# A two-layer hybrid mixing block: a fourth buffer for two weight rings, spectra products from split parts, and an early output projection in two rounds

## The chip, the cores and the metric

The kernel runs on one core of one Trainium2 chip. The metric is the device time of one execution in microseconds; it is told as the median of several runs. The engines are named as in the profile: PE is TensorE (matmul; PEld its weight loads), DVE is VectorE, ACT is ScalarE, POOL is GpSimd, SP is SyncE, which here only issues transfers.

## The reference

Two layers work on 512 latent tokens and 256 context tokens of width 1024. Each layer has a token mixing part with four groups of heads, which share an input and an output projection, and a feed-forward part. In short:

```python
for l in range(2):
    need_ctx = l < 1
    mod  = silu(c) @ ada_w[l] + ada_b[l]          # shifts, scales, gains; the same for ctx
    h, hc = modulate(rmsnorm(x)), modulate(rmsnorm(ctx))
    pl, pc = h @ w_in, hc @ w_in                  # 1024 -> 2400
    # four groups of 256 columns of the mixed result
    y = concat(s5(pl, pc), hyena(pl), retention(pl, pc), mla(pl, pc)) @ w_out
    x = x + g1 * rmsnorm(y)
    x = x + g2 * rmsnorm(conv_ffn(modulate(rmsnorm(x))))   # w_up 1024x5632, conv, silu gate, w_down
    # the same for ctx in layer 0
# hyena: z = x1 * long_conv(v, 0); z = x2 * long_conv(z, 1), with filter spectra
def hyena_spectra(n, w1, b1, w2, b2, w3, freq, deltas):
    hid = sin(freq * (z @ w1 + b1));  hid = sin(freq * (hid @ w2 + b2))   # 64 wide
    k = (hid @ w3) * exp(-t01 * abs(deltas))      # n x (2 orders x 2 directions x 256)
    k = k * rsqrt(sum(k * k)); return rfft(two_sided(k))
```

All values are float32.

## The kernel before, in words

Activations stand transposed, with channels on partitions and tokens along the free axis: segment 0 is the context (256 tokens), segment 1 the latents (512). A dense product takes weights of 128x128 as the stationary side and tokens as the moving side.

**Split products.** A float32 matmul of the tensor engine is slow, so most large products are made from split parts in the type F32R. `load_w` (line 308) brings a weight block of 128x1024 (512 KB) from memory into the raw ring "wr" (`load_raw`, line 299), ACT casts it to a high part "wh" (`split_w`, line 305), and DVE subtracts to get the low part "wl" (line 306). "wr", "wh" and "wl" have three buffers each. Activations are split in the same manner into H1h and H1l (latents), H0h and H0l (context). `passes` (line 320) gives three products for each block k: wh by high, wh by low, wl by high. `dense` (line 329, its products on line 341) is built on it. Weight loads are issued at a raised priority, so that they go ahead of other work in the order. A second ring, "ar", of three buffers of 128x1024 too, holds adaLN weights (`ada`, line 461; its products on line 482), the Fourier tables of the hyena part (lines 822 and 880) and some others.

**What sets the order.** The code is written as Python generators that take turns (`weave`, `ahead`): a list of input projection jobs, a chain with retention, S5 and the context's hyena part, a chain with latent attention (MLA) and, in layer 0, the latents' hyena part, the spectra, and the adaLN products. How many steps each takes in a turn is a table of small numbers. From what is written this way a scheduler lays out one list of instructions for each engine, and an engine works its list off in order: an instruction that waits holds all behind it. Nearly all transfers are issued by SP, in SP's order; GpSimd issues the loads of S5's operands (lines 991 and 992) and some of MLA's (lines 1379 and 1381).

**Spectra** (`hy_spectra`, line 744). Two small products with a sine after each give the hidden layer h2 of 64 rows and n columns. For both orders, w3 (64x512) is loaded, and for each of the T2 = n/128 token blocks one float32 product (line 790) makes 128x512 filter values, which are multiplied by a window, squared and summed, normed, and transformed. This is done for the context and the latents of layer 0 beside the input projection of layer 0 (60 to 340 us), and for the latents of layer 1 beside the feed-forward part of layer 0 (912 to 1003 us).

**The hyena loop** (line 879). For each pair of frequencies a table tb comes into "ar", a spectrum kt from memory; lines 890 and 891 transform forwards, DVE multiplies (lines 894 to 899), and `back` (lines 872 and 873) transforms back for the pair before.

**S5's readout** reloads what it stored before (lines 1075 and 1076, tiles A_U and A_T) and works on it on DVE (line 1077).

**The early output projection** (`early_out`, line 1816, its products on line 1827). When the results of a head group stand in C (the split tiles H1h, H1l, H0h, H0l of the mixed result, blocks k: 0 and 1 S5, 2 and 3 hyena, 4 and 5 retention, 6 and 7 MLA), part of the output projection can be done. In layer 0, where `stage[0]` is set, this starts when all of KP = (4, 5, 0, 1, 6, 7) is filled. Three blocks of w_out are loaded, and seven sums of 18 products of 256 columns each are begun in four PSUM tiles, 126 products. The blocks 2 and 3 and the rest of the columns follow in the main output projection (line 1898).

The scratch for descriptors of GpSimd's transfers has its default size, since the program's constructor names none; it lies in the on-chip memory that the pools share.

## Time and profile before

| | us |
|---|---|
| three runs | 2066.98, 2062.43, 2060.63 |
| median | 2062.43 |
| the profiled execution | 2065.18 |
| its span | 2063.4 |
| TensorE busy | 1891.1 (92%) |
| VectorE busy | 1330.3 (64%) |
| ScalarE busy | 791.3 (38%) |
| GpSimd busy | 173.3 (8%) |
| mean granted clock of TensorE | 0.951 |

Busy time is summed over the instructions of an engine; the granted clock is a share of full speed, so 1.00 stands for 2.4 GHz and 0.50 for 1.2 GHz, and values between are means over a stretch. The stages of the span: 0 to 340 us adaLN and the input projection of layer 0 with spectra, S5's preparation and retention beside it; 340 to 612 us the rest of mixing in layer 0 (MLA, S5, hyena, early output projection); to about 710 us the output projection; then the feed-forward part of layer 0 until about 1240 us; mixing of layer 1 until about 1690 us; its feed-forward part to the end. Idle time in the profile stands in brackets at the instruction that came after it, with what released it.

### The profile page before, as it was taken

How to read it: one execution, taken by the hardware profiler on the slowest of the kernel's cores; microseconds unless marked ns; L12 is line 12 of the kernel's file. 1: busy time of each engine (PE TensorE's matmuls, PEld its weight loads, DVE VectorE, ACT ScalarE, POOL GpSimd, SP SyncE). 2: the span in 40 equal slices, each digit the busy share in tenths (PEclk: the TensorE clock that was granted, in tenths of full speed). 3: DMA queues.
4: the chain of work that ended last, by engine and by line, in shares of the span. 5: the costliest groups of instructions: out<-in, count | busy, mean ns of one | idle time of the engine just before them, and what ended most of it. 6: DMA issues, size and time to landing. Idle time of an engine off the chain costs nothing. (4 is left out here: it accounts for less than half of the span.)

```text
span 2063.4 us, 29216 instructions
## 1 busy us (share of the span) xinstructions
PE 1891.1 (92%) x11142; PEld 1554.8 (75%) x11142; DVE 1330.3 (64%) x2488; ACT 791.3 (38%) x1351; POOL 173.3 (8%) x195
## 2 busy tenths in 40 slices
PE   6898999887899899999999998889989979999996
PEld 1766666566698788878888887678867968888885
DVE  4767463686746897776788447538767555555555
ACT  3646312343334434352523233433355534333332
POOL 0221004100001002100000001110022000000001
PEclk8899999889999999999999999899989989999998
DMA  8557456635452543333277222486621423333331
GB/s 287 179 191 236 159 167 181 152 84 159 133 175 93 195 126 114 123 97 103 87 276 253 64 77 74 117 213 197 196 84 51 144 88 116 103 92 102 93 102 41
DMA packets 147411, 284.96 MB, mean 138 GB/s; under 512 B 35429, under 2 KB 78598, under 8 KB 147272
## 3 DMA queue, kind: packets, MB, share of 16 engines
q1 hardware_dynamic: 139592, 274.70, 41.8%
q0 software_dynamic: 3072, 7.08, 2.0%
q10 hardware_dynamic: 4608, 1.31, 0.3%
q8 instruction: 88, 1.44, 0.3%
q14 instruction: 51, 0.42, 0.1%
HBM read 231.17 MB, written 48.99 MB: 136 GB/s over the span
## 5 line engine op out<-in xcount | busy, mean ns | idle before, releaser
L306 DVE TENSOR_TENSOR wl<-wr,wh 128x1024 fp32r<-128x1024 f32 x174 | 214.0, 1232 | 262.4 <-ACT wh L305 259.7
L341 PE MATMUL mm<-H1h,wh 128*128 128x512 f32 x888 | 354.8, 399 | 5.5 <-DVE st L426 4.5
L341 PE MATMUL mm<-H1h,wl 128*128 128x512 f32 x888 | 353.8, 399 | 0.3 <-DVE wl L306 0.3
L341 PE MATMUL mm<-H1l,wh 128*128 128x512 f32 x888 | 351.8, 396 | 0.0
L305 ACT CAST wh<-wr 128x1024 fp32r<-128x1024 f32 x174 | 182.2, 1050 | 354.6 <-PE mm L341 295.2
L341 PEld LDWEIGHTS mm<-H1h,wh 128*128 128x128 f32 x888 | 168.4, 190 | 47.0 <-issue 6.5
L341 PEld LDWEIGHTS mm<-H1l,wh 128*128 128x128 f32 x888 | 168.0, 189 | 38.7 <-issue 2.6
L341 PEld LDWEIGHTS mm<-H1h,wl 128*128 128x128 f32 x888 | 168.2, 189 | 37.2 <-issue 0.8
L341 PE MATMUL mm<-H0h,wh 128*128 128x256 f32 x480 | 137.0, 285 | 9.9 <-DVE st L426 9.9
L404 POOL TENSOR_TENSOR rq_y<-rq_v,halves 128x2 f32<-128x2 f32 (+3 forms) x37 | 36.0, 972 | 1233.8 <-DVE rq_v L403 736.9
L341 PE MATMUL mm<-H0l,wh 128*128 128x256 f32 x480 | 138.2, 288 | 0.0
L341 PE MATMUL mm<-H0h,wl 128*128 128x256 f32 x480 | 138.0, 288 | 0.0
L341 PE MATMUL mm<-ff_mh,wh 128*128 128x512 f32 (+1 forms) x432 | 131.7, 356 | 0.9 <-DVE y L1959 0.7
L341 PE MATMUL mm<-ff_mh,wl 128*128 128x512 f32 (+1 forms) x432 | 132.4, 358 | 0.0
L341 PE MATMUL mm<-ff_ml,wh 128*128 128x512 f32 (+1 forms) x432 | 131.2, 355 | 0.0
L341 PEld LDWEIGHTS mm<-H0h,wh 128*128 128x128 f32 x480 | 92.3, 192 | 14.1 <-issue 13.0
L341 PEld LDWEIGHTS mm<-H0l,wh 128*128 128x128 f32 x480 | 91.7, 191 | 7.3 <-issue 6.8
L341 PEld LDWEIGHTS mm<-H0h,wl 128*128 128x128 f32 x480 | 92.0, 192 | 4.0 <-issue 3.7
L424 ACT ACTIVATE st<-mm,c_ffn_v 128x512 f32<-128x512 f32 (+1 forms) x132 | 88.1, 700 | 1.7 <-PE mm L356 1.7
L1959 DVE TENSOR_TENSOR y<-mm,y 128x512 f32<-128x512 f32 x80 | 53.5, 686 | 54.5 <-PE mm L341 54.4
L426 DVE SCALAR_TENSOR_TENSOR st<-mm,c_ffn_v,st 128x511 f32<-128x511 f32 (+1 forms) x132 | 83.1, 654 | 1.4
L341 PEld LDWEIGHTS mm<-ff_mh,wh 128*128 128x128 f32 x432 | 72.2, 188 | 14.9 <-DVE y L1959 1.2
(610 smaller groups left out, 4162.4 us busy)
## 6 DMA issues: line engine op xcount, KB each, us to landing
wr<-in_w_up SPq DMA_DIRECT2D x88, 512.0 KB, 3.7
ada_w<-in_ada_t SPq DMA_DIRECT2D x49, 512.0 KB, 5.3
wr<-in_w_down SPq DMA_DIRECT2D x44, 512.0 KB, 3.4
ar<-in_ada_w SPq DMA_DIRECT2D x40, 512.0 KB, 5.9
wr<-in_w_in SPq DMA_DIRECT2D x34, 512.0 KB, 6.2
ar<-in_k_tabl SPq DMA_DIRECT2D x16, 512.0 KB, 3.8
wr<-in_w_out SPq DMA_DIRECT2D x16, 512.0 KB, 4.3
xs_d<-x SPq DMA_DIRECT2D x8, 1024.0 KB, 5.3
```

Of the source, the lines that this page charges most:

```text
L305: act.copy(hi, raw)
L306: dve.tensor_tensor(lo, raw, hi.bitcast(F32), ALU.subtract)
L341: pe.matmul(outs[s], w, X(k, s, j), start=f, stop=z)
L404: pool.tensor_tensor(y, v, halves[:, :n], ALU.pow)
L424: act.activation(u[:, o:o + m], ps, AF.Identity, bias=vw[:, 3:4], scale=vw[:, 1:2])
L426: dve.scalar_tensor_tensor(u[:, o:o + m - 1], ps[:, 1:m], vw[:, 2:3], u[:, o:o + m - 1], ALU.mult, ALU.add)
L1959: dve.tensor_tensor(d, ps, d, ALU.add)
```

## The change

Three things are changed. (1) The rings "wr" and "ar" have four buffers instead of three. The 8 KB per partition for that, and 4 KB for new tiles of the spectra, come from the descriptor scratch, which is set to 4096 bytes. (2) In `hy_spectra` h2 is split into hh (128 rows: high part above, low part below, F32R). w3 is loaded twice, into both halves of a tile of the "ar" ring, cast to wh (128 rows) and split to wl (64 rows). The one float32 product becomes two F32R products: hh by wh with 128 rows, which gives high by high and low by high, and the high half by wl with 64 rows. (3) `early_out` has two rounds, KP = ((4, 5, 6, 7), (0, 1)): it may start when retention and MLA are filled, makes their 84 products, and waits for S5 before it makes the other 42. It hands over after its 6th and 12th product of a sum and no longer after the 9th and 18th. The main output projection takes the blocks in the order 4, 5, 6, 7, 0, 1, 2, 3 where it makes a whole sum.

```diff
--- before.py
+++ after.py
@@ -297,7 +297,7 @@
 
 
     def load_raw(src, n=1024):
-        raw = new(wp, [128, 1024], "wr", bufs=3)
+        raw = new(wp, [128, 1024], "wr", bufs=4)
         qw.dma_start(raw[:, :n], src)
         return raw
 
@@ -465,7 +465,7 @@
         def load(k):
             raws = []
             for h in range(2):
-                raw = new(wp, [128, 1024], "wr" if early and h else "ar", bufs=3)
+                raw = new(wp, [128, 1024], "wr" if early and h else "ar", bufs=4)
                 qa.dma_start(raw, I["ada_w"][b, k, h])
                 raws.append(raw)
             return raws
...
@@ -766,7 +766,8 @@
             act.activation(o, a, AF.Sin)
 
         h1 = new(p, [64, n], "y_win")
-        h2 = new(p, [64, n], "y_h2")
+        h2 = new(p, [64, n], "y_S")
+        hh = new(p, [128, n], "y_h2", F32R)
         ps = sm_ps()
         pe.matmul(ps[0:64, :n], w12[0:33, 0], pz, start=True, stop=True)
         sine(ps[0:64, :n], hs[:, 0:1], h1)
@@ -774,10 +775,17 @@
         ps = sm_ps()
         pe.matmul(ps[0:64, :n], w12[:, 1], h1, start=True, stop=True)
         sine(ps[0:64, :n], hs[:, 1:2], h2)
+        act.copy(hh[0:64], h2)
+        dve.tensor_tensor(hh[64:128], h2, hh.bitcast(F32)[0:64], ALU.subtract)
         yield
         for o in range(2):
-            w3 = new(p, [64, 512], "y_kt")
-            sp.dma_start(w3, I["hy_w3"][l, o])
+
+            w3 = new(wp, [128, 512], "ar", bufs=4)
+            for r in (0, 64):
+                sp.dma_start(w3[r:r + 64], I["hy_w3"][l, o])
+            wh, wl = new(p, [128, 512], "y_w3h", F32R), new(p, [64, 512], "y_w3l", F32R)
+            act.copy(wh, w3)
+            dve.tensor_tensor(wl, w3[0:64], wh.bitcast(F32)[0:64], ALU.subtract)
             dl = new(p, [128, 512], "f_s")
             sp.dma_start(dl, I["hy_d"][l:l + 1, o * 512:(o + 1) * 512].to_broadcast([128, 512]))
             act.activation(dl, dl, AF.Abs)
@@ -787,7 +795,8 @@
                 win = new(p, [128, 512], "y_win")
                 act.activation(win, dl, AF.Exp, scale=nt[:, c:c + 1])
                 ps = sm_ps()
-                pe.matmul(ps, h2[:, c * 128:(c + 1) * 128], w3, start=True, stop=True)
+                pe.matmul(ps, hh[:, c * 128:(c + 1) * 128], wh, start=True, stop=False)
+                pe.matmul(ps, hh[0:64, c * 128:(c + 1) * 128], wl, start=False, stop=True)
                 dve.tensor_tensor(kk[:, c], ps, win, ALU.mult)
                 if c == 0:
                     act.activation(acc, kk[:, c], AF.Square)
...
@@ -858,7 +867,7 @@
 
         def pair():
             t = new(p, [128, 2, 2, 256], tg["pr"]) if tg["pr"] else \
-                new(wp, [128, 1024], "wr", bufs=3).rearrange("p (x a b) -> p x a b", x=2, a=2)
+                new(wp, [128, 1024], "wr", bufs=4).rearrange("p (x a b) -> p x a b", x=2, a=2)
             return t[:, 0], t[:, 1]
 
         gp = planes(al, z, R)
...
@@ -1643,7 +1652,7 @@
 
         C = None
         Wo, outp, early_m = [], {}, set()
-        KP, KR = (4, 5, 0, 1, 6, 7), (2, 3)
+        KP, KR = ((4, 5, 6, 7), (0, 1)), (2, 3)
         KI = {"cat5": 0, "cath": 2, "catr": 4, "catm": 6}
         early, filled = {}, set()
 
@@ -1818,15 +1827,18 @@
                 for m in range(3):
                     Wo.append(load_w(fl(I["w_out"][l, m])))
                 yield
-                for m, (s, h) in [(m, x) for x in subs for m in range(2)] + [(2, subs[0])]:
-                    if m % 2 == 0:
-                        outp[s, h, m // 2] = mm_ps()
-                    d = outp[s, h, m // 2][:, (m % 2) * 256:(m % 2) * 256 + 256]
-                    early_m.add((s, h, m))
-                    for i, (w, k, j, f, z) in enumerate(passes(blk(Wo[m]), KP)):
-                        pe.matmul(d, w, C[s][j][:, k, h:h + 256], start=f and m % 2 == 0, stop=False)
-                        if i in FILL:
-                            yield
+                for i, ks in enumerate(KP):
+                    while not all((k, s) in filled for k in ks for s in segs):
+                        yield
+                    for m, (s, h) in [(m, x) for x in subs for m in range(2)] + [(2, subs[0])]:
+                        if i == 0 and m % 2 == 0:
+                            outp[s, h, m // 2] = mm_ps()
+                        d = outp[s, h, m // 2][:, (m % 2) * 256:(m % 2) * 256 + 256]
+                        early_m.add((s, h, m))
+                        for j_, (w, k, j, f, z) in enumerate(passes(blk(Wo[m]), ks)):
+                            pe.matmul(d, w, C[s][j][:, k, h:h + 256], start=f and i == 0 and m % 2 == 0, stop=False)
+                            if j_ in (5, 11):
+                                yield
 
             def ahead():
 
@@ -1859,7 +1871,7 @@
                     gC = gC or collect()
                     if not run(gC, 1):
                         gC = False
-                if stage[0] and gT is not False and all((k, s) in filled for k in KP for s in segs):
+                if stage[0] and gT is not False and all((k, s) in filled for k in KP[0] for s in segs):
                     gT = gT or early_out()
                     if not run(gT, W_T):
                         gT = False
...
@@ -2047,7 +2059,7 @@
     from concourse.bass_utils import run_bass_kernel_spmd
 
     arrays = _layout(inputs)
-    nc = bacc.Bacc("TRN2", target_bir_lowering=False, num_devices=1)
+    nc = bacc.Bacc("TRN2", target_bir_lowering=False, num_devices=1, dynamic_dma_scratch_size=4096)
     _build(nc, arrays)
     r = run_bass_kernel_spmd(nc, [{"in_" + k: v for k, v in arrays.items()}], core_ids=[0])
     o = r.results[0]["out_x"]
```

TensorE's order in the hyena loop, before the change, around the second table's forward products (L890 and L891; L953 and the like are others' work, L872 and L873 `back`):

```order
L890 MATMUL sm_4486<-st_4483,ar_4475 128x256
L891 MATMUL sm_4486<-st_4483,ar_4475 128x256
L1048 MATMUL sm_4449<-A_HS_4410,A_CA_4396 128x32
L1049 MATMUL sm_4449<-A_HS_4410,A_CA_4396 128x64
L890 MATMUL sm_4521<-st_4518,ar_4514 128x256
L891 MATMUL sm_4521<-st_4518,ar_4514 128x256
L890 MATMUL sm_4521<-st_4518,ar_4514 128x256
L891 MATMUL sm_4521<-st_4518,ar_4514 128x256
L872 MATMUL sm_4532<-st_4494,ar_4475 128x256
L873 MATMUL sm_4532<-st_4494,ar_4475 128x256
```

And with the change, where the line numbers are nine to twelve higher (L899 and L900 forwards, L881 and L882 backwards, L1839 the early output projection); the dots stand for 23 more rows of L1839:

```order
L899 MATMUL sm_4542<-st_4539,ar_4531 128x256
L900 MATMUL sm_4542<-st_4539,ar_4531 128x256
L1057 MATMUL sm_4505<-A_HS_4448,A_CA_4434 128x32
L1058 MATMUL sm_4505<-A_HS_4448,A_CA_4434 128x64
L1839 MATMUL mm_4808<-H1h_3318,wh_4495 128x256
L1839 MATMUL mm_4808<-H1l_3319,wh_4495 128x256
L1839 MATMUL mm_4808<-H1h_3318,wl_4496 128x256
...
L1839 MATMUL mm_5048<-H1h_3318,wl_4502 128x256
L1839 MATMUL mm_5048<-H1h_3318,wh_4501 128x256
L899 MATMUL sm_4584<-st_4581,ar_4577 128x256
L900 MATMUL sm_4584<-st_4581,ar_4577 128x256
L899 MATMUL sm_4584<-st_4581,ar_4577 128x256
```

The second table's forward products, which stood right behind the first table's, now have 28 products of the early output projection ahead of them.

SyncE's order, before, around the load of S5's stored output (L1076; L881 loads a table, L884 a spectrum, L964 a convolution's operand):

```order
L884 DMA A_GT_4885<-hy_Kc_103 128x768
L884 DMA B_Q_4578<-hy_K_23_101 128x768
L881 DMA ar_4576<-in_k_tabl 128x1024
L881 DMA ar_4641<-in_k_tabl 128x1024
L1076 DMA A_T_4569<-s_y_28_106 128x768
L884 DMA B_Q_4643<-hy_K_23_101 128x768
L884 DMA B_Q_4679<-hy_K_23_101 128x768
L881 DMA ar_4677<-in_k_tabl 128x1024
L881 DMA ar_4702<-in_k_tabl 128x1024
```

And with the change (L1085 that load, L890 a table, L893 a spectrum, L973 the operand):

```order
L893 DMA A_GT_4945<-hy_Kc_103 128x768
L893 DMA B_Q_4647<-hy_K_23_101 128x768
L890 DMA ar_4716<-in_k_tabl 128x1024
L890 DMA ar_4758<-in_k_tabl 128x1024
L1085 DMA A_T_4638<-s_y_28_106 128x768
L893 DMA B_Q_4718<-hy_K_23_101 128x768
L893 DMA B_Q_4760<-hy_K_23_101 128x768
L890 DMA ar_4783<-in_k_tabl 128x1024
L890 DMA ar_4826<-in_k_tabl 128x1024
```

Two table loads stand ahead of the S5 load in both; they are the fourth and fifth table of the two hyena convolutions before, and the fifth and sixth with the change, since a fourth table is loaded further ahead.

SyncE's order in layer 1's input projection, before (L301 loads a raw weight, L1001 and L981 serve S5, L1737 stores hyena operands, L884 loads a spectrum):

```order
L301 DMA wr_12147<-in_w_in 128x1024
L1001 DMA A_r_2023_11775<-s_rot_22_100 128x576
L1737 DMA pd_3_68_146<-st_11845 128x512
L301 DMA wr_12324<-in_w_in 128x1024
L1737 DMA pd_4_69_147<-st_11917 128x512
L301 DMA wr_12512<-in_w_in 128x1024
L884 DMA h_kt_12218<-hy_K_24_102 128x768
L1737 DMA pd_5_70_148<-st_11992 128x512
L884 DMA h_kt_12240<-hy_K_24_102 128x768
L301 DMA wr_12687<-in_w_v 128x1024
L301 DMA wr_12693<-in_w_v 128x1024
L301 DMA wr_12887<-in_w_in 128x1024
```

And with the change (L1010 and L1746 for L1001 and L1737, L893 for L884):

```order
L1746 DMA pd_3_68_146<-st_11904 128x512
L301 DMA wr_12383<-in_w_in 128x1024
L301 DMA wr_12571<-in_w_in 128x1024
L1746 DMA pd_4_69_147<-st_11976 128x512
L893 DMA h_kt_12277<-hy_K_24_102 128x768
L893 DMA h_kt_12299<-hy_K_24_102 128x768
L1746 DMA pd_5_70_148<-st_12051 128x512
L301 DMA wr_12746<-in_w_v 128x1024
L301 DMA wr_12752<-in_w_v 128x1024
L301 DMA wr_12946<-in_w_in 128x1024
L301 DMA wr_12988<-in_w_in 128x1024
```

Two weight loads now stand in a row ahead of the store into pd_4, where one stood before, and two w_in loads stand behind those of w_v, where one stood.

## Rows read from the trace of the kernel before

**Rows 1.** Stretches: length, busy us (instructions) by engine, clock, DMA share, GB/s

```profile
50.00:340.00 290.00, 265.75 (x1541) 200.60 (x1542) 187.78 (x369) 123.50 (x227) 52.67 (x39) 0.94 0.58 186
340.00:484.00 144.00, 123.72 (x900) 92.43 (x900) 98.41 (x277) 53.49 (x144) 19.19 (x39) 0.88 0.52 127
484.00:549.00 65.00, 44.47 (x193) 35.02 (x189) 40.31 (x85) 17.71 (x30) 0.00 (x0) 0.87 0.49 159
549.00:585.00 36.00, 35.34 (x228) 32.31 (x227) 26.61 (x56) 9.07 (x17) 0.00 (x0) 1.00 0.50 159
910.00:1240.00 330.00, 327.70 (x1826) 280.16 (x1825) 216.58 (x353) 112.26 (x147) 2.31 (x2) 1.00 0.42 138
1340.00:1394.00 54.00, 43.75 (x268) 37.85 (x269) 21.41 (x32) 15.91 (x25) 6.27 (x13) 0.91 0.83 216
```

**Rows 2.** Waits of ScalarE over the whole run: total, times, longest

```profile
ACT wh L305 <- PE mm L341: 295.2, 111, 9.9
...
ACT wh L305 <- DMA wr<-in_w_in: 18.2, 5, 7.6
```

**Rows 3.** Timeline of TensorE in layer 0's feed-forward part: start, duration, operation

```profile
911.22 0.39 PE L341 MATMUL mm<-H1l,wh 128*128 128x512 f32 x1
...
911.45 0.28 PE L341 MATMUL mm<-H0l,wh 128*128 128x256 f32 x1
...
915.47 1.98 PE L790 MATMUL sm<-y_kt,y_h 64*128 64x512 f32 x4
...
917.38 0.50 PE L341 MATMUL mm<-H1l,wh 128*128 128x512 f32 x1
```

**Rows 4.** Groups by form: count, busy us, mean ns, idle time before

```profile
L790 PE MATMUL sm<-y_kt,y_h 64*128 64x512 f32 x40 | 20.1, 618 | 0.0
...
L397 ACT CAST ff_mh<-st 128x512 fp32r<-128x512 f32 x22 | 13.7, 620 | 52.8 <-DVE st L1975 52.8
```

**Rows 5.** Timeline of TensorE, the early output projection

```profile
549.86 0.28 PE L1827 MATMUL mm<-H1l,wh 128*128 128x256 f32 x1
...
549.97 0.29 PE L1827 MATMUL mm<-H1h,wl 128*128 128x256 f32 x1
```

**Rows 6.** Timeline of TensorE in the hyena loop; in brackets idle time and releaser

```profile
496.14 1.19 PE L890 MATMUL sm<-st,ar 128*128 128x256 f32 x2 [3.01 <-DVE st L740]
...
512.75 1.19 PE L890 MATMUL sm<-st,ar 128*128 128x256 f32 x2 [6.67 <-DVE st L740]
...
529.17 1.19 PE L890 MATMUL sm<-st,ar 128*128 128x256 f32 x2 [6.19 <-issue]
...
541.70 0.67 PE L890 MATMUL sm<-st,ar 128*128 128x256 f32 x2 [2.31 <-issue]
```

**Rows 7.** Timeline of SyncE (SP) and VectorE (DVE) before 512.75

```profile
501.86 3.29 SPq L881 DMA_DIRECT2D ar<-in_k_tabl  x2
...
507.02 0.33 SPq L1076 DMA_DIRECT2D A_T<-s_y  x1
...
510.62 1.02 DVE L1077 SCALAR_TENSOR_TENSOR A_T<-A_T,c_vec 128x768 f32<-128x768 f32 x1 [3.21 <-DMA A_T<-s_y]
```

**Rows 8.** Waits of TensorE, 0 to 340 us

```profile
PE sm L482 <- DMA ar<-in_ada_w: 6.8, 6, 1.9
```

**Rows 9.** Waits of ScalarE and TensorE, 1340 to 1394 us

```profile
ACT wh L305 <- DMA wr<-in_w_in: 17.2, 3, 7.6
...
PE mm L341 <- DVE st L426: 9.3, 2, 8.9
```

**Rows 10.** Timeline of GpSimd's (POOL) S5 loads in layer 1 and of their first reader

```profile
1344.81 3.33 POOL L991 DMA_DIRECT2D A_U<-s_u  x6 [16.28 <-DMA s_u<-st]
...
1356.01 0.56 POOL L992 DMA_DIRECT2D A_T<-s_T  x1 [1.02 <-DMA A_U<-s_u]
...
1388.35 1.54 PE L1009 MATMUL sm<-A_U,A_SB 128*64 128x96 f32 x32
```

**Rows 11.** DMA issues: count, KB each, median us to landing

```profile
A_U<-s_u POOLq DMA_DIRECT2D x16, 128.0 KB, 8.7
```

More of the change, by code (lines that the diff above doesn't have):

```diff
@@ L485, in ada @@
             yield
-        row = new(wp, [128, 512], "ar", bufs=3)
+        row = new(wp, [128, 512], "ar", bufs=4)
         act.copy(row, ps)
@@ L821, in hy_spectra @@
                 nb = 5 if cl == 0 else 3
-                tb = new(wp, [128, 1024], "ar", bufs=3)
+                tb = new(wp, [128, 1024], "ar", bufs=4)
                 sp.dma_start(tb[:, :nb * 128], I["k_spt" + nmx][cl, :, :nb * 128])
@@ L879, in long_conv @@
         for cl in range(R // 2):
-            tb = new(wp, [128, 1024], "ar", bufs=3)
+            tb = new(wp, [128, 1024], "ar", bufs=4)
             qh.dma_start(tb, I["k_tab" + nmx][cl])
@@ L942, in hyena @@
             g = tg["v" if w else "x1"]
-            t = new(p, [128, T2, 256], g) if g else new(wp, [128, 1024], "wr", bufs=3).rearrange("p (a b) -> p a b", a=4)
+            t = new(p, [128, T2, 256], g) if g else new(wp, [128, 1024], "wr", bufs=4).rearrange("p (a b) -> p a b", a=4)
             us = []
@@ L1269, in lent @@
             if alt in ("wr", "ar"):
-                return new(wp, shape, alt, bufs=3)
+                return new(wp, shape, alt, bufs=4)
             return new(p, shape, alt, dt, bufs=2)
@@ L1896, in tile_kernel @@
                             e = (s, h, 2 * m2 + m) in early_m
-                            for w, k, j, f, z in passes(blk(W[2 * m2 + m]), KR if e else KP + KR):
+                            for w, k, j, f, z in passes(blk(W[2 * m2 + m]), KR if e else KP[0] + KP[1] + KR):
                                 pe.matmul(ps[:, m * 256:(m + 1) * 256], w, C[s][j][:, k, h:h + 256],
```

## The prediction

> **What bounds the kernel now.** I read first the table of busy times by stretch, then the idle times of TensorE and what ended them, then the queues of SyncE and GpSimd where one of these idle times points to them.
>
> The table of stretches [rows 1] separates two kinds of time. From 910 to 1240 us, in layer 0's feed-forward part, TensorE (PE) is busy 327.70 of 330 us at a granted clock of 1.00: there a change is worth just the PE time that it removes, and a weight that arrives earlier is worth nothing. The mixing stages are different: 340 to 484 us has 123.72 of 144 us, 484 to 549 us 44.47 of 65 us at clock 0.87, and 1340 to 1394 us 43.75 of 54 us at 0.91. There PE waits, and its clock falls after waits. 549 to 585 us is full again (35.34 of 36).
>
> The whole-run waits of ScalarE (ACT) on its weight casts [rows 2] say which buffer holds the weight stream: 295.2 us wait for PE, that is for a free split buffer (three each of "wh" and "wl", unchanged), and only 18.2 us for a raw input-projection weight to land. So a fourth raw buffer can only help where such DMA waits are: layer 0's start and layer 1's input projection.
>
> **Part 1, spectra from split parts.** One fp32 product of 64x128x512 becomes two F32R products of the same 512 columns. A spectra pass makes T2 products for each of 2 orders: 4 for the context, 8 for layer 0's latents, 8 for layer 1's, so 20, which are the 40 records of the group [rows 4] (two each). In the trace four records, two products, start at 915.47 and the next instruction starts at 917.38 [rows 3]: 0.95 us a product, with the entry into it; without that I take 0.85. An F32R product with 512 columns starts at 911.22 and the next one at 911.45, so 0.23 us, and two make 0.47 [rows 3]. Saved: 0.38 us x 20 = 7.6 us. Eight products lie in the full feed-forward stretch and give their 3.0 us whole; twelve lie beside layer 0's input projection, where PE is busy 265.75 of 290 us [rows 1], so 4.6 us x 0.92 = 4.2. Together 7.
>
> What it adds: per order one ACT cast of 128x512 (0.62 us by the row of such casts), one VectorE (DVE) subtract of 64x512 (half as many elements; I take 0.62 again), and per pass a cast and a subtract of the hidden layer: 9 casts and 9 subtracts, at most 5.6 us on each engine [rows 4]. ACT and DVE have slack in both places (DVE 216.58 of 330 us, 187.78 of 290). If that cover were gone the sum would lose at most 5.6 us, and that is my bound. The hidden layer's split lies between the second sine and the first product, some 1.2 us later, where PE has weights to multiply. On SyncE's queue (SP) there are 6 more loads, about 0.4 us each, 2.4 us over two long stretches: nothing. They also sit in the "ar" ring now, which takes part of the fourth slot away where spectra and adaLN weights run together; I charge that to part 3.
>
> **Part 2, the early output projection in two rounds.** It is 126 products of 256 columns. In the trace they start 0.12 us apart (549.86, 549.97) [rows 5], 15.1 us in all, between 549 and 585 where PE has no idle time. The change starts the retention and latent-attention round before the hyena part, and the S5 round later. Its place in PE's order: 37 products in the end of the attention part, 14 among S5's, 28 ahead of the first long wait of the hyena loop, 5 ahead of a short one, 12 and 15 ahead of two later long ones, 15 near the end. The hyena idle times that matter [rows 6] are 3.01 us (496.14), 6.67 (512.75), 6.19 (529.17) and 2.31 us (541.70). Into them go 28 x 0.12 = 3.4 us against 3.01, so 3.0; 1.4 against 6.19; 1.8 against 2.31; nothing stands in front of the 6.67. The 51 earlier ones, 6.1 us, go into a stretch with 144 - 123.72 = 20.3 us idle; a product there also stands in front of attention work that is itself on the chain, so I count half, 3.0. Absorbed: 3.0 + 1.4 + 1.8 + 3.0 = 9.2 us. But 549 to 585 then meets DVE, which is busy 26.61 of its 36 us: it can't shrink by more than 9.4. I take 8. Bounds: the granted clock is 0.87 in 484 to 549; at 1.00 its 44.47 busy us would take 44.47 x 0.13 = 5.8 us less, so -14 at best. The other end: the product batches come just before the released hyena pairs and push the chain PE, DVE, PE by their own lengths (3.4 + 1.4 + 1.8 = 6.6 us), and the shorter stretch behind pays only 9.4 back: about -3.
>
> The 6.67 stays. It ends on DVE, whose L740 stood behind L1077, and that waited 3.2 us for an S5 output load that SP issued at 507.02, behind two table loads held 3.29 us for a buffer [rows 7]. A fourth table buffer sounds like the cure, but in SP's new order the same load stands behind the fifth and sixth table instead of the fourth and fifth; with four slots the sixth waits for table 2, as the fifth did with three. So nothing.
>
> **Part 3, the rings.** At the start PE waits 6.8 us in all for adaLN weights from the "ar" ring in layer 0's input projection [rows 8]. One more slot lets a load go out earlier; half of that, little of it lost to the spectra's use of the slots, is -3 (bounds 0 and -6). In layer 1's input projection ACT waits 17.2 us in three pieces for raw weights, and PE 9.3 us, 8.9 of them in one piece, for a result of the same chain [rows 9]. SP's order there brings each weight load one weight ahead of the hyena and S5 transfers. DMA is already 0.83 busy there [rows 1], so the loads mostly share bandwidth rather than use idle time: I take -4, less than half of 9.3, with +2 (the weights push the S5 loads back) and -9 as bounds. The feed-forward stretches get nothing by rows 1 and 2.
>
> **Sum.** -7 - 8 - 3 - 4 = -22. The profiled execution took 2065.18 us, 2063.4 of span and 1.8 around it, and lies 2.7 us above the median of 2062.43, inside the runs' 2060.6 to 2067.0. So 2065.2 - 22 = 2043 us. All terms at their good bounds give -7.6 - 14 - 6 - 9, so 2029; at their bad ones (part 1 less its 5.6) -1.4 - 3 - 0 + 2, so about 2063.
>
> **A rule of the skill against the trace.** The shrunken scratch serves the loads that GpSimd issues. The trace shows these: 128 KB loads issued 0.56 us apart (six in 3.33 us at 1344.81) that land after a median of 8.7 us [rows 10, 11], so about 8.7/0.56 = 15 are in flight. The Trainium skill ("DMA: Bandwidth & Descriptors", section "SWDGE vs HWDGE vs iDMA") says that descriptors of such transfers are written to rings in a carved-out part of SBUF, and "SBUF — State Buffer" (section "SBUF size: 192, 224, or 256?") gives 16 KiB for it; no run here shows either yet. By that 4096 bytes is a quarter, an estimate of four in flight. The first of these pages, in its section "Anatomy of one DMA — SWDGE (gpsimd) path", fits a fixed 2.0 us plus bytes over 436 GB/s, an estimate of 2.3 us for 128 KB; the 8.7 us measured beside other traffic disagrees, and the measurement decides. By the page's figure eleven loads one after the other would be through at 1344.8 + 25 = 1370, ahead of their reader; by the row they would not, which is the second rival.
>
> **Rivals.** *Rings and rounds do nothing* (0.14): the split buffers bind [rows 2], the waits in the hyena loop reopen because their length is set by the chain over DVE and DMA, and what leaves 549 to 585 only makes PE wait there. Then part 1 alone remains: 2065.2 - 7 = 2058, no change. For it: 295.2 against 18.2 us. Against it: the filled places are PE's own idle time, which products that wait for nothing do use.
>
> *Slower: the smaller scratch makes GpSimd wait for room* (0.10). Place: layer 1's S5 loads. Eleven are issued from 1344.81 on, and their first reader, L1009, starts at 1388.35 [rows 10]. If only one at a time were in flight, they take 11 x 8.7 = 96 us, end at 1440 and hold the S5 chain by 52 us; of this attention and hyena work would cover little, since PE idles only for what S5 feeds, and at 45 us less the gain of 22 the time is 2088. With four in flight it is 24 us, done at 1369, and free. So it decides below two in flight: above 4 us between GpSimd's issues it costs. Against it: the trace has some fifteen in flight, far above two, and shows no wait for room.
>
> *More than the sum* (0.08): the filled waits also keep the clock at 1.00 through 484 to 549 and layer 1's wait of 8.9 us goes: about 2025.
>
> **How the numbers follow.** The forecast has 0.68, with a range of its own from 2030 to 2056. A measurement of this kernel can't tell less than about 0.3% (6.2 us) from no change, so faster means below 2056.2 and slower above 2068.6. Faster: 0.68 and 0.08, so 0.76; within: 0.14; slower: 0.10. The range of 2024 to 2064 leaves out the slower rival, the upper part of the first and a tail below, some 0.18.
>
> **What would show it.** Right: in the new profile the spectra's products pace at 0.23 us; PE's early products lie between 440 and 545, with those idle times of 3.01, 6.19 and 2.31 us gone or shorter by 3.0, 1.4 and 1.8 us and 6.67 still there; the stretch that was 549 to 585 is 26 to 30 us long; layer 1's raw-weight waits are shorter than their 17.2 us; both feed-forward stretches unchanged but for 3 us. Wrong: GpSimd's issues wider than 0.56 us or L1009 in layer 1 later against its surroundings; ACT or DVE waits that newly end on the w3 loads; or PE idle in the attention part grown by what the early products took.

## The result, and the profile after

The changed kernel takes 2041.91 us (median of four runs, 2040.97 to 2044.83) against 2063.64 for the kernel before on the same chip. The ratio is 0.9887, with a 95% interval from 0.9866 to 0.9908: faster by 1.1%, and 21.7 us by the medians. A second set gave 2043.57 us and a ratio of 0.9899 [0.9882, 0.9916]. The forecast was 2043 with a range of 2024 to 2064. The sum was right; several of its terms were not, as shown below.

The table of stretches of the changed kernel, each moved to the same place in the work as in [rows 1] (length, busy us and instructions by engine, clock, DMA share, GB/s):

```profile
50.00:334.60 284.60, 263.04 (x1589) 202.92 (x1590) 194.88 (x376) 129.10 (x236) 53.40 (x41) 0.95 0.60 198
334.60:476.30 141.70, 123.24 (x889) 94.22 (x889) 100.32 (x277) 55.24 (x145) 17.37 (x38) 0.87 0.47 119
476.30:538.50 62.20, 51.67 (x270) 43.30 (x266) 40.56 (x86) 16.27 (x28) 0.00 (x0) 0.92 0.48 152
538.50:569.00 30.50, 25.51 (x136) 21.01 (x134) 22.84 (x52) 7.34 (x15) 0.00 (x0) 1.00 0.54 171
892.00:1222.00 330.00, 326.51 (x1826) 280.67 (x1825) 217.43 (x355) 113.37 (x149) 3.07 (x2) 1.00 0.41 139
1324.00:1374.60 50.60, 44.34 (x272) 38.59 (x272) 21.50 (x32) 15.29 (x25) 6.29 (x13) 0.93 0.81 223
```

Beside [rows 1]: the hyena stretch (third row) has TensorE busy 51.67 of 62.2 us instead of 44.47 of 65, and its clock rose from 0.87 to 0.92. The stretch behind it (fourth row) is 30.5 us long instead of 36, so both together take 92.7 us instead of 101. The attention part before (second row) has 18.5 us of idle time where it had 20.3. Layer 0's feed-forward part (fifth row) lost only 1.2 us of TensorE's busy time in 330. Layer 1's input projection (sixth row) waits 6.3 us instead of 10.3.

To see where the 21.7 us came from, cut both executions at the same products: the start of the 1000th, the 3500th and the 4000th record of line 341, TensorE's dense products. The first stretch is all of layer 0's mixing and a little of the next part, the second most of its feed-forward part, the third layer 1's mixing. The kernel before:

```profile
0.00:743.10 743.10, 647.78 (x3999) 500.09 (x4000) 485.75 (x1046) 291.52 (x566) 87.39 (x97) 0.93 0.55 171
743.10:1223.60 480.50, 475.43 (x2701) 405.06 (x2700) 337.59 (x568) 175.98 (x244) 21.64 (x14) 1.00 0.41 131
1223.60:1699.70 476.10, 420.46 (x2824) 360.91 (x2823) 304.65 (x621) 195.13 (x377) 57.77 (x78) 0.92 0.43 128
```

And the changed one:

```profile
0.00:725.60 725.60, 639.13 (x4000) 500.64 (x4001) 493.03 (x1053) 296.43 (x575) 86.30 (x97) 0.93 0.55 177
725.60:1206.00 480.40, 474.54 (x2701) 405.32 (x2700) 339.70 (x571) 177.52 (x247) 22.40 (x14) 1.00 0.41 133
1206.00:1678.50 472.50, 420.98 (x2824) 361.45 (x2823) 303.46 (x619) 195.31 (x377) 57.71 (x78) 0.92 0.43 127
```

Layer 0's mixing gained 17.5 us (743.1 to 725.6), of which 8.7 are TensorE's busy time and 8.8 idle time. The feed-forward stretch gained 0.1, layer 1's mixing 3.6. The last 2.3 us of the profiled spans' difference (23.5) arose behind the third cut, nearly all of it after the last instruction of VectorE: from there to the end it is 5.6 us before and 3.3 with the change. GpSimd ends the program with drains, sequencer instructions that the profile lists under line 2041 (2053 with the change). Here they are, before and after (count, ns min/median/max, first and last start):

```profile
L2041 POOLq DRAIN  x3: 46/102/6620, 2056.0 to 2063.1; - x3
```

```profile
L2053 POOLq DRAIN  x3: 40/102/3430, 2034.7 to 2039.6; - x3
```

The longest drain takes 6.62 us in both kernels here with the default scratch (the kernel before and the one with the early projection alone) and 2.9 to 3.4 us in all twelve executions with 4096 bytes. So about 2 us of the gain belong to the smaller scratch itself, to which the prediction gave none. No kernel here changes the scratch alone; this is read from the ends of the traces.

The spectra's new products, TensorE and its weight loads (PEld) in the feed-forward part of the changed kernel:

```profile
898.64 0.19 PEld L798 LDWEIGHTS sm<-y_w3h,y_h 128*128 128x128 f32 x1
...
898.76 0.40 PE L798 MATMUL sm<-y_w3h,y_h 128*128 128x512 f32 x1
...
899.08 0.18 PEld L799 LDWEIGHTS sm<-y_w3l,y_h 64*128 64x128 f32 x1 [0.26 <-issue]
...
899.08 0.49 PE L799 MATMUL sm<-y_w3l,y_h 64*128 64x512 f32 x1
...
899.51 0.19 PEld L798 LDWEIGHTS sm<-y_w3h,y_h 128*128 128x128 f32 x1 [0.24 <-issue]
...
899.51 0.50 PE L798 MATMUL sm<-y_w3h,y_h 128*128 128x512 f32 x1
...
900.37 0.50 PE L341 MATMUL mm<-H1h,wl 128*128 128x512 f32 x1
```

Four products take 1.61 us from 898.76 to 900.37; the four records of the float32 form took 1.91 [rows 3]. From product to product it is 0.43 us, not the 0.23 of the forecast. The PEld rows show why: from the second product on, a weight load starts no earlier than the record of its own product (both at 899.08, then 899.51), with PEld idle 0.24 to 0.26 us before it. The load at 898.64 starts 0.12 us ahead of its product (898.76), while the dense product before it still runs.

It is not the smaller number of rows by itself. In the attention part products with 96 rows follow one another at full pace, 0.12 us for 256 columns, as those with 128 rows do [rows 5]:

```profile
462.21 0.28 PE L1378 MATMUL mm<-wl,B_Q 96*128 96x256 f32 x1
462.33 0.29 PE L1379 MATMUL mm<-wh,B_R 96*128 96x256 f32 x1
462.46 0.28 PE L1377 MATMUL mm<-wh,B_Q 96*128 96x256 f32 x1
```

TensorE in the hyena loop of the changed kernel, to be read against [rows 6]:

```profile
488.67 0.60 PE L899 MATMUL sm<-st,ar 128*128 128x256 f32 x2
...
503.43 1.19 PE L899 MATMUL sm<-st,ar 128*128 128x256 f32 x2 [6.00 <-DVE st L740]
...
517.34 0.62 PE L1839 MATMUL mm<-H1h,wh 128*128 128x256 f32 x3 [3.54 <-ACT H1h L397]
...
520.11 1.07 PE L899 MATMUL sm<-st,ar 128*128 128x256 f32 x2
...
531.18 0.70 PE L899 MATMUL sm<-st,ar 128*128 128x256 f32 x2
```

The second pair (488.67) comes without a wait, where there were 3.01 us, and so does the seventh (531.18), where there were 2.31. The 6.67 before the fourth is 6.00 now. The fifth (520.11) no longer waits 6.19 us, but a new wait of 3.54 us stands ahead of it: the first product of the S5 round waits for ACT's cast of the S5 result.

### The profile page after: what moved, and what is told of

The parts are those of the page before. It is cut to its first block, busy times and chain, and to the rows that moved or that the text cites. A ratio compares the mean times of both kernels' runs of the same rounds, so it can differ in the third digit from the quotient of the medians.

```text
span 2039.9 us, 29242 instructions
## 1 busy us (share of the span) xinstructions
PE 1881.6 (92%) x11142; PEld 1556.2 (76%) x11142; DVE 1338.5 (66%) x2497; ACT 798.0 (39%) x1362; POOL 172.9 (8%) x195
```

## The experiments

Ratios are to the kernel before, timed beside each, with 95% intervals, and the gains in us are worked out from them. All kernels here but the early projection alone have the scratch of 4096 bytes, so their gains hold the 2 us or so at the program's end.

**Part 1 alone** (rings of three, one-round projection).

```diff
+            wh, wl = new(p, [128, 512], "y_w3h", F32R), new(p, [64, 512], "y_w3l", F32R)
...
-                pe.matmul(ps, h2[:, c * 128:(c + 1) * 128], w3, start=True, stop=True)
+                pe.matmul(ps, hh[:, c * 128:(c + 1) * 128], wh, start=True, stop=False)
+                pe.matmul(ps, hh[0:64, c * 128:(c + 1) * 128], wl, start=False, stop=True)
```

> Part 1 alone: split spectra, rings of three buffers, one-round early projection, scratch of 4096 bytes. The trace of the changed kernel shows the F32R products of the spectra 0.43 us apart instead of the 0.23 that was forecast, since the weight load of each waits for the product before it; so four products take 1.6 us where four records of the float32 form took 1.9, and with the edges one float32 product replaced saves 0.2 us. Theory (a part is worth its product time where TensorE is full, 20 x 0.2): 4 us faster, about 2059.5 against 2063.6; 1.6 us of it in the feed-forward part of layer 0. Rival (the forecast's size, 0.38 each): 7 us faster. Second rival (the w3 loads take a slot of the table ring from the adaLN weights, which the fourth buffer hides in the full change): no gain or up to 3 us slower, with longer waits of the adaLN products (L482).

Measured 2055.02 us, ratio 0.9967 [0.9952, 0.9981], so 6.8 us faster, from 3.9 to 9.9. Its trace (an execution of 2060.3 us) has the attention part begin 2.8 us earlier and nothing gained in the feed-forward stretch (481.9 us long, 480.5 before, at a clock a little lower). Only 5.3 us of the gain are in this trace: 1.4 in layer 0's mixing, -1.4 in its feed-forward part, 3.0 in layer 1's mixing, where there are no spectra products, and 2.2 at the end. So the 6.8 us are not shown to be the spectra's; without the end some 4.6 are left. The interval holds both the 4 and the 7 that were expected. The second rival falls: TensorE's waits for adaLN weights are 3.9 us there, not longer than the 6.8 before.

**Part 3 alone, and each ring alone.** Both rings, then the table ring, then the raw ring with four buffers; the same lines with one number:

```diff
-        raw = new(wp, [128, 1024], "wr", bufs=3)
+        raw = new(wp, [128, 1024], "wr", bufs=4)
...
-            tb = new(wp, [128, 1024], "ar", bufs=3)
+            tb = new(wp, [128, 1024], "ar", bufs=4)
```

> Part 3 alone: both rings with four buffers, scratch of 4096 bytes. Theory: faster by 9 us, 5 of them before the attention part of layer 0 (adaLN and raw weights of the input projection) and 4 in layer 1's input projection, where TensorE's 8.9 us wait shrinks to about 5. Rival (the split buffers bind, the ring does nothing): within 2 us of before. The smaller scratch should show nothing: GpSimd's issues stay 0.56 us apart.

> Only the ring of tables and adaLN weights (ar) has four buffers; scratch 4096 bytes. Both rings alone gave 12.4 us. Theory (most of that is the adaLN products of layer 0's input projection, whose weights wait for a slot of this ring, 6.8 us of TensorE waits and the slow clock behind them): 6 to 8 us faster, the attention part of layer 0 beginning 6 to 8 us earlier, nothing in layer 1. Rival (raw weights were late): under 3 us.

> Only the raw weight ring (wr) has four buffers; scratch 4096 bytes. Theory: 4 to 6 us faster, in layer 1's input projection (2 to 3 us) and at the start, where half of the first adaLN weights come through this ring. Rival (raw ring carries the gain of both): 9 us or more; then the attention part of layer 0 begins 8 us earlier with this ring alone.

Both: 2052.12 us, 0.9940 [0.9925, 0.9955], 12.4 us faster. The table ring alone: 2051.91 us, 0.9938 [0.9920, 0.9956], 12.8 us. The raw ring alone: 2061.57 us, 0.9976 [0.9964, 0.9989], 5.0 us. So the table ring carries as much as both, and more than the 6 to 8 us expected of it. The raw ring's 5.0 us lies in its expected 4 to 6, but with the end taken off some 3 us are left of it. The attention part begins 9.4, 9.0 and 2.1 us earlier. TensorE's waits for adaLN weights of that ring up to 368 us, with the table ring at four and then with the raw ring at four:

```profile
PE sm L482 <- DMA ar<-in_ada_w: 1.9, 3, 1.5
```

```profile
PE sm L482 <- DMA ar<-in_ada_w: 6.1, 6, 1.4
```

**Part 2 alone.** The rounds, with rings of three:

```diff
-        KP, KR = (4, 5, 0, 1, 6, 7), (2, 3)
+        KP, KR = ((4, 5, 6, 7), (0, 1)), (2, 3)
...
+                for i, ks in enumerate(KP):
+                    while not all((k, s) in filled for k in ks for s in segs):
+                        yield
```

> Part 2 alone: the early output projection in two rounds, rings of three, default scratch. Theory: 8 us faster, all between the start of the latents' hyena loop and the main output projection; TensorE's waits of 3.0, 6.2 and 2.3 us there gone or shorter, the 6.7 us one still there. Rival (the waits reopen because they are set by the chain over VectorE and the transfers, and the fourth buffers are what let the products fill them): less than 3 us faster.

Measured 2057.47 us, 0.9968 [0.9956, 0.9980]: 6.6 us faster, 4.1 to 9.1. In its trace the hyena loop begins 1.1 us earlier than before and the next stage's first product (L356) 8.8 us earlier, so 7.7 us arise just where they were expected. The rival's 3 us is out.

**128 rows in both spectra products**, on top of the full change:

```diff
-            wh, wl = new(p, [128, 512], "y_w3h", F32R), new(p, [64, 512], "y_w3l", F32R)
+            wh, wl = new(p, [128, 512], "y_w3h", F32R), new(p, [128, 512], "y_w3l", F32R)
...
-            dve.tensor_tensor(wl, w3[0:64], wh.bitcast(F32)[0:64], ALU.subtract)
+            dve.tensor_tensor(wl, w3, wh.bitcast(F32), ALU.subtract)
...
-                pe.matmul(ps, hh[0:64, c * 128:(c + 1) * 128], wl, start=False, stop=True)
+                pe.matmul(ps, hh[:, c * 128:(c + 1) * 128], wl, start=False, stop=True)
```

> The full change, with the low part of w3 kept for both halves (wl of 128 rows), so that both spectra products have 128 rows; it computes the product of the two low parts in addition. Theory (the weight load is exposed because neighbouring products differ in rows, 64 and 128): the spectra products come 0.23 us apart, 20 x 2 x 0.2 us of TensorE time less, so up to 8 us less, 3 of them sure in the feed-forward part; about 2037 to 2039 against the full change's 2041.9. Rival (the weight load is exposed for another reason, such as the 512-column product into a bank of its own): pace stays 0.43 and the time within 1 us of the full change.

> The full change with 128-row spectra products once more, beside the two below on one chip. Theory: 2 to 4 us under the full change (2041.9 and 2043.6 in two sets), so 2039 to 2040, ratio to before about 0.988.

TensorE's spectra products in this kernel, in the same place of the feed-forward part:

```profile
896.50 0.40 PE L798 MATMUL sm<-y_w3h,y_h 128*128 128x512 f32 x1
...
896.74 0.40 PE L799 MATMUL sm<-y_w3l,y_h 128*128 128x512 f32 x1
...
896.97 0.39 PE L798 MATMUL sm<-y_w3h,y_h 128*128 128x512 f32 x1
...
897.20 0.39 PE L799 MATMUL sm<-y_w3l,y_h 128*128 128x512 f32 x1
...
897.43 0.39 PE L341 MATMUL mm<-H1h,wl 128*128 128x512 f32 x1
```

Four products take 0.93 us, 0.23 each, and the next dense product follows at the same distance. So the pace of 0.43 came from products of 64 rows among those of 128, and by the 96-row products above from the change and not from the fewer rows. The time: 2039.49 us, 0.9882 [0.9862, 0.9901], and again 2040.72 us, 0.9876 [0.9856, 0.9896]. That is 2 to 3 us under the full change by the medians, inside both intervals, so the mechanism is shown and its worth in the whole time only likely. In the feed-forward stretch it can be seen where the clock stayed at 1.00, as in the kernel with five table buffers below, between the same products:

```profile
717.50:1194.70 477.20, 471.03 (x2701) 405.62 (x2700) 338.88 (x571) 177.35 (x247) 22.40 (x14) 1.00 0.41 134
```

It is 477.2 us long instead of 480.5, about the 3.0 us that the prediction gave this stretch.

**The memory of the raw ring's fourth buffer, given back or to the table ring**, on top of that:

```diff
-        raw = new(wp, [128, 1024], "wr", bufs=4)
+        raw = new(wp, [128, 1024], "wr", bufs=3)
...
-            tb = new(wp, [128, 1024], "ar", bufs=4)
+            tb = new(wp, [128, 1024], "ar", bufs=5)
```

> As k128_again, with the raw weight ring (wr) back at three buffers and the table ring (ar) at four. Alone, four table buffers gave as much (12.8 us) as both rings (12.4). Theory (the fourth raw buffer carries nothing that the split buffers don't hold back): within 2 us of k128_again, with layer 1's input projection waiting 2 to 3 us longer for raw weights and the attention part of layer 0 beginning at the same time. Rival (in the full order the raw ring matters, as it did alone by 5 us): 4 us or more slower than k128_again.

> The same memory spent the other way: wr three buffers, ar five. Theory (with four the adaLN products of layer 0 hardly wait any more, 1.9 to 2.9 us of 6.8 left, so a fifth buffer has little left to take): 0 to 3 us faster than with four table buffers, by an earlier start of the attention part. Rival (each buffer takes a like share): 6 us or more faster. Third: tables of the hyena loop are loaded before they are wanted and crowd the queue of SyncE ahead of S5's loads: slower by 2 us or more, seen as a longer wait before the fourth forward products of the hyena loop.

Three raw and four table buffers: 2038.74 us, 0.9859 [0.9834, 0.9884], no slower than with four raw ones (2040.72 in the same set). Three and five: 2033.38 us, 0.9839 [0.9816, 0.9862], 7.3 us under 2040.72. The attention part begins 7.0 us earlier than in the execution with four and four (357.3 against 364.4). The cleaner comparison, with three raw buffers on both sides, gives 5.4 us (2038.74 less 2033.38) at overlapping intervals, which lies between the theory's 0 to 3 and the rival's 6 or more; neither is settled. If the gain is real, it did not come out of the waits that I had counted: those that name this ring are 2.8 us in the execution with four and four, 3.3 with three and four and 3.1 with three and five. The third possibility, a time longer by 2 us or more, is out.

**S5's readout loads on GpSimd's queue**, on top of the 128-row kernel with four buffers in both rings, and of the one with three raw and five table buffers:

```diff
-            qc.dma_start(t[:, :, n0:], s5_y[l][128 * i:128 * i + 128][:, :, n0:])
+            pool.dma_start(t[:, :, n0:], s5_y[l][128 * i:128 * i + 128][:, :, n0:])
```

The load of s5_u on the line above is moved in the same way.

> The full change with 128-row spectra products, and the loads of S5's stored output and input (tiles A_U and A_T of the readout) issued by GpSimd instead of SyncE, in both layers. The prediction says that the wait of 6.7 us in the hyena loop (6.0 with the change) stays because that load stands behind two table loads that wait for a buffer. Theory: issued on a queue that is idle there, it lands some 5 to 10 us earlier, VectorE's wait of 2.5 us before L1086 and TensorE's 6.0 us before the fourth forward products go, and the S5 results are split earlier, so that TensorE's 3.5 us before the second round goes too: 5 to 8 us faster than the 128-row kernel's 2039.5, so about 2033. Rival (VectorE's chain through the pairs sets the pace, the load was merely the last to be waited for): TensorE waits as long for the chain as before and less than 2 us is gained.

> The fastest so far (wr three, ar five buffers, 128-row spectra products; 2033.4 us, ratio 0.984) with S5's readout loads on GpSimd's queue. With four table buffers that move gave no measurable gain, since the load's own data, a store of S5, landed only then, and the chain over VectorE kept 4.2 us of TensorE's wait. Theory: again nothing, within 2 us of 2033. Rival (five tables queued ahead make SyncE hold the load longer, so that the other queue now pays): 3 to 5 us faster, about 2029.

With four: 2039.75 us, 0.9877 [0.9858, 0.9897], as without it (0.9882 and 0.9876). Its load of A_T on GpSimd, the DVE instruction behind it, and then TensorE's wait before the fourth pair (total, times, longest):

```profile
488.65 0.55 POOL L1085 DMA_DIRECT2D A_T<-s_y  x1 [12.21 <-DMA s_y<-A_Y]
...
493.31 1.02 DVE L1086 SCALAR_TENSOR_TENSOR A_T<-A_T,c_vec 128x768 f32<-128x768 f32 x1 [0.70 <-DMA A_T<-s_y]
```

```profile
PE sm L899 <- DVE st L740: 4.2, 1, 4.2
```

GpSimd, with nothing else to do, waits 12.21 us for the store that the load reads. TensorE's wait was 6.5 and 7.4 us in the two executions of the 128-row kernel without the move, so 2 to 3 us of it went in this execution. The larger part stays, since the S5 result itself comes late. With five: 2028.77 us, 0.9830 [0.9810, 0.9851], the fastest run here, 36 us under its own set's 2064.96; TensorE's wait is 6.6 us there and 5.9 without the move, so it was not shortened at all, and the 4.6 us against 2033.38 (another set, overlapping intervals) can't be put down to it.

**The full change again:**

> The full change again, beside the others on the same chip, for a direct comparison. Theory (the three parts add up, since they lie in different stretches): spectra 6.8, rings 12.4 and early projection 6.6 us, 25.8 in sum less some 2 us of overlap in the input projection, so 23 to 25 us faster than before. Rival (they share the same idle times): under 20 us.

2043.57 us, 20.9 us faster by the ratio [17.3, 24.4], an interval that reaches into the theory's 23 to 25 and into the rival's under 20 alike. The three parts alone sum to 25.8 us (ratios multiplied: 0.9876). The two sets of the full change gave 23.3 and 20.9, so the parts add up but for some 2 to 5 us. About 2 of these are the scratch's, which the sum counts twice, with the spectra and with the rings.

## Why the prediction was right, and where it was not

*Spectra, 7 us: wrong in its working, and the 6.8 measured alone does not bear it out.* Some 2 of the 6.8 us are the scratch's. The step that failed is "an F32R product ... 0.23 us, and two make 0.47". That pace was read from neighbours that all have 128 rows. With 64 and 128 rows in turn two make 0.8, and two float32 products replaced save 1.91 - 1.61 = 0.30 us, so 0.15 each instead of 0.38. With the edges, where the float32 products also cost 0.1 us, it is 0.2 each. The feed-forward stretch, put at 3.0 us, gave 0.1 by the cut at the same products. TensorE's busy time fell by 0.9 us there (475.43 to 474.54) and its idle time rose by 0.8, for which one new wait is enough:

```profile
1039.94 0.39 PE L341 MATMUL mm<-ff_mh,wh 128*128 128x256 f32 x1 [1.06 <-DVE y L1971]
```

All seven executions with four raw buffers have it, none of the seven with three. So the raw ring's fourth buffer comes with a cost of 1 us in a stretch for which the prediction saw no effect of the rings.

*Early projection, 8 us: right.* Alone it gave 6.6. The places were as said: TensorE's early products run from 465 to 543 us, and the 3.01 and 2.31 us went. The stretch behind shrank to 30.5 us, just outside the 26 to 30 that were said; with the hyena stretch it is 8.3 us less (101 to 92.7). One detail differs: the 6.19 went wholly, but 3.54 came back at the S5 round, a wait that the order of the changed kernel shows (12 products ahead of the pair) and the prediction did not price.

*The 6.67 stays: right, for a reason that holds at most in part.* I put it down to two table loads ahead of the S5 load. On a free queue the load waits for S5's store all the same, and 4.2 us of TensorE's wait stay, 6.6 with five table buffers.

*Rings, 3 and 4 us: the mis-sized terms.* The start was put at half of 6.8 us of waits. The row that answers in the changed kernel, from TensorE's waits up to 368 us:

```profile
PE sm L482 <- DMA ar<-in_ada_w: 2.9, 3, 2.0
```

So 3.9 us of these waits went, near the 3 forecast, but the waits are not what was gained. They fell to 3.9 us with the spectra alone too, in a ring of three. The attention part begins 8.7 us earlier, and 9.0 with the table ring alone. TensorE up to the attention part's first product (L1368, L1377) before the change, with the table ring alone, and with the full change:

```profile
0.00:376.36 376.36, 334.33 (x1886) 231.40 (x1886) 222.59 (x470) 150.44 (x271) 64.22 (x61) 0.94 0.63 201
```

```profile
0.00:367.38 367.38, 326.95 (x1886) 228.12 (x1887) 224.27 (x473) 152.34 (x275) 66.55 (x64) 0.95 0.64 209
```

```profile
0.00:367.63 367.63, 323.57 (x1887) 230.75 (x1887) 230.98 (x480) 156.78 (x283) 67.78 (x69) 0.94 0.66 215
```

With the table ring alone TensorE makes the same products, and 7.4 of the 9.0 us are its busy time; its idle time fell by only 1.6 us (42.0 to 40.4). With the full change its idle time is 44.1 us, 2 more than before. So as the waits on this ring went, others took their place (those for a sine's result before L776 come to 5.7 us now), and what was gained is that the same products ran faster, at a mean clock of 0.95 instead of 0.94 with the ring alone. The sum had no term for the pace. Which wait, or which change of order, raised it is not settled.

In layer 1 the waits went as said in the profiled execution. ACT's waits for raw weights, then TensorE's, in the changed kernel, against [rows 9]:

```profile
ACT wh L305 <- DMA wr<-in_w_v: 13.1, 1, 13.1
...
ACT wh L305 <- DMA wr<-in_w_in: 4.2, 2, 3.3
...
PE mm L341 <- DVE st L426: 5.3, 1, 5.3
```

The input weights wait 4.2 instead of 17.2 us, the next ones (w_v) 13.1 instead of 7.7, so the wait in part moved on, and TensorE's is 5.3. But the 128-row kernel with the same two rings shows, in its second set:

```profile
PE mm L341 <- DVE st L426: 10.3, 1, 10.3
```

Over the seven executions with four raw buffers the longest such wait is 5.3 to 10.3 us, 7.7 in the mean; over the seven with three it is 8.1 to 9.2, 8.9 in the mean. The whole of layer 1's mixing, between the same products, takes 474.5 us in the mean of either group. So the changed kernel's 3.6 us there can't be put down to the raw ring, whose 4 us are not borne out, and a kernel with three raw buffers is no slower.

*The sum* came out partly by luck. Layer 0's mixing was to gain some 15 us by its terms (4.2, 8 and 3) and gained 17.5; the feed-forward part was to gain 3.0 and gave 0.1; layer 1 gave about its 4 in this execution, but not by the fourth raw buffer; and 2 us came at the end, where none had been looked for.

*The slower rival fell.* GpSimd's loads in layer 1 of the changed kernel, the five in a row and the last of the group:

```profile
1328.23 2.77 POOL L1000 DMA_DIRECT2D A_U<-s_u  x5 [0.39 <-issue]
...
1338.14 0.56 POOL L1001 DMA_DIRECT2D A_T<-s_T  x1 [0.56 <-DMA A_U<-s_u]
```

And their landing (count, KB, median us):

```profile
A_U<-s_u POOLq DMA_DIRECT2D x16, 128.0 KB, 8.7
```

Five in 2.77 us are 0.55 us apiece, and 8.7 us is the same landing time as before [rows 10, 11]. The first reader (L1018) starts at 1368.83, 19.5 us earlier than before, as its surroundings do. With the scratch at 4096 bytes nothing on GpSimd waits for room; how small it may get was not tried. The prediction's fifteen in flight was too many: before the change, GpSimd issued eight of these loads and then waited for one of them to land.

```profile
1353.17 0.56 POOL L992 DMA_DIRECT2D A_T<-s_T  x1 [3.93 <-DMA A_U<-s_u]
```

What the Trainium skill states in "DMA: Bandwidth & Descriptors" (section "SWDGE vs HWDGE vs iDMA"), that such descriptors lie in rings in SBUF, is neither shown nor denied by that. *Rings and rounds do nothing* fell with 12.4 and 6.6 us alone, also with 2 us taken off the first.

## What to carry to other kernels

Read the pace of a product from neighbours of its own shape: where rows alternate, the weight load shows. Count a buffer's worth by a run with one buffer of that ring more, ring by ring: waits that name the ring gave 3 us where the next part began 9 earlier, and half of the memory went to a ring whose fourth buffer showed no gain beside the other's. Where a change comes with a setting of its own, as the scratch here, run that setting alone too, or its worth is counted with each part. Work that is ready can fill an engine's waits only if the order puts it in front of them and its own inputs are there in time.

## What was not expected of the hardware

A short wait in a full stretch costs more than itself. In the execution with both rings alone, TensorE in the feed-forward part:

```profile
889.65 1.04 PE L771 MATMUL sm<-y_S,y_w 33*64 33x512 f32 x2 [1.91 <-ACT st L1974]
```

And the stretch around it:

```profile
850.00:900.00 50.00, 48.09 (x279) 40.18 (x278) 37.99 (x57) 24.53 (x37) 0.42 (x4) 0.97 0.47 135
```

The clock was 1.00 there in the kernel before, whose wait at this line is 1.1 us, and 0.97 here. From 891 to 894 us it is 0.50, the lower of the two levels, and products of 512 columns then take 0.43 us instead of 0.23. The feed-forward stretch is 484.7 us long instead of 480.5. The one with the early projection alone has a wait of 2.0 us at this line, a clock of 0.93, and 485.6. By the same products, 2.3 of the 4.2 us and 4.0 of the 5.1 arise within the ten us around this wait, which itself is only 0.8 and 0.9 us longer than before. Its length alone does not tell when this happens: 1.4 us at this place left the clock at 1.00 in the kernel with three raw and five table buffers, and 1.2 us came with a clock of 0.91 over the 20 us around it in the one with S5's loads moved. Of the rest with both rings most comes with the wait of 1.06 us that four raw buffers bring; with the early projection it is not settled. A stage in which the early projection has no work so moved by nearly as much as that part gained.

The program's end depends on GpSimd's scratch for descriptors: the closing drain took 6.62 us with the default size and 2.9 to 3.4 us with 4096 bytes.
